# The w_down product of a two-layer encoder as seven half-size products, on one Trainium2 core

## The chip, the cores and the metric

The kernel runs on one core of one Trainium2 chip. A core has TensorE (PE in the profile; its weight loads are shown apart as PEld), VectorE (DVE), ScalarE (ACT), GpSimd (POOL) and SyncE (SP), which issues most DMAs. The metric is the device time of one execution in microseconds; differences are judged by the median of several runs.

## The reference

Two layers over 512 tokens of width 1024. Each layer adds an attention mixer and then a squared-relu MLP; a final RMSNorm follows. Layer 0's mixer joins forgetting attention and chunked attention with a relative bias; layer 1's joins stick-breaking attention and latent attention. The change is in the MLP:

```python
def rmsnorm(x, g):
    xf = x.astype(jnp.float32)
    y = xf * lax.rsqrt(jnp.mean(xf * xf, axis=-1, keepdims=True) + EPS)
    return (y * g.astype(jnp.float32)).astype(x.dtype)

def squared_relu_mlp(h, w_up, w_down):
    return jnp.square(jax.nn.relu(h @ w_up)) @ w_down

for layer in range(DEPTH):
    h = rmsnorm(x, norm_mix[layer])
...
    x = x + squared_relu_mlp(rmsnorm(x, norm_mlp[layer]), w_up[layer], w_down[layer])
return rmsnorm(x, norm_final)
```

All is float32; w_up is 1024 by 4096 and w_down 4096 by 1024 in each layer.

## The kernel before, in words

**Precision.** Every operand of a matmul is split into a high part (a cast to float32r) and the rest: ScalarE casts, VectorE subtracts (`load_w`, lines 429 to 461, for weights). `mm3` (line 423) then issues three matmuls: high by high, high by low, low by high. A matmul loads 128 by 128 elements and streams up to 512 columns into a bank of PSUM.

**Tiles.** X, the residual, is four token tiles of 128 by 1024. `norm_T` (line 533) multiplies X by the gain and transposes it on TensorE into eight chunks of 128 features by 512 tokens. For the MLP it leaves out the token's own scale: it returns one over the mean square for each token tile, and `add_proj` multiplies by it when it adds into X.

**The MLP** (`mlp`, line 753) goes over eight groups of four chunks of the 4096 hidden features. `up_group` makes a group: for each pair of 128-feature blocks two loads of w_up (512 KB each), then for each block 8 chunks by three matmuls; ScalarE takes the relu from the bank, VectorE multiplies it by the bank's relu again, and the square is split. `add_proj` (line 723) multiplies a group by its rows of w_down: for each half of the 1024 columns and each token tile, 4 chunks by three matmuls, and VectorE adds the bank into X with the scale. `up_group` of the next group is recorded ahead of `add_proj` of this one.

**What sets the order.** The program doesn't issue instructions directly: `Plan` (lines 58 to 226) records them, works out their dependencies, and lays them out by a list schedule: on each engine the ready operation of the lowest record number goes first (`urgent` lowers that by `BOOST`). Its clock is a table of durations (`Op.cost`, line 302) and of latencies between engines. A tile is placed only when its pool has a free buffer and, save in pool `u`, when all tiles of its tag that were recorded earlier have been placed. Each engine then runs its instructions in that order, whatever the chip does.

**Buffers.** `wp` holds the halves of weights (tags `wh` and `wl`, four each) and two raw tiles; `tp` seven tiles of 128 by 512 for transposed attention weights; `low_keys` are three tiles that live for the whole program (line 481); `ex` three scratch tiles; PSUM's eight banks are three `mm`, two `sc`, two `tr`, one `av`.

Nearly every instruction is issued from line 225, so the profile's groups are told apart by the names of tiles: `wh`, `wl` are halves of weights, `wr` raw weights, `u` activations, `mm` a bank of a projection, `ex` scratch, `p`, `k`, `pt` attention weights.

Of the kernel before, what the change touches and what calls it, by code (L numbers as in the profile page):

```python
# [17 lines left out]
P = 128  # L18
S = 512
# [3 lines left out]
EPS = 1e-6  # L23
BOOST = 4000
WARM = 60
WARM2 = 12
# [260 lines left out]
class Op:  # L287
# [38 lines left out]

# [44 lines left out]
def trunk(ctx, tc, x, positions, norm_mix, norm_mlp, norm_final, w_in_ab, b_forget, rel_bias,  # L371
# [50 lines left out]

    def mm3(ps, a, b, first, last):

        nc.tensor.matmul(ps, lhsT=a[0], rhs=b[0], start=first, stop=False)
        nc.tensor.matmul(ps, lhsT=a[0], rhs=b[1], start=False, stop=False)
        nc.tensor.matmul(ps, lhsT=a[1], rhs=b[0], start=False, stop=last)

    def load_w(view, parts=None, place="w", raw_place="w"):


        n = int(np.prod(view.shape[1:]))
        if raw_place == "hd":
            raw = hp.tile([P, 1024], F32, tag="hd", name=nm("wr"))
        else:
            raw = wp.tile([P, 1024], F32, tag="wr", name=nm("wr"), bufs=2)
        if place == "hd":
            hi, lo = (hp.tile([P, 1024], F32R, tag="hd", name=nm(s)) for s in ("wh", "wl"))
        elif place == "pt":
            hi, lo = (tp.tile([P, S], F32R, tag="pt", name=nm(s)) for s in ("wh", "wl"))  # L440
        else:
            hi = wp.tile([P, 1024], F32R, tag="wh", name=nm("wh"))
            lo = wp.tile([P, 1024], F32R, tag="wl", name=nm("wl"))
# [32 lines left out]
    for _ in range(WARM):  # L476
        nc.tensor.matmul(warm[:, 0:P], lhsT=idle, rhs=idle, start=True, stop=True)

    low_keys = [cp.tile([P, 2, S], F32R, name=f"KL{i}") for i in range(3)]
    for t in low_keys:
        nc.gpsimd.memset(t[64:128, 0].bitcast(F32), 0.0)
        nc.vector.memset(t[0:64, 1].bitcast(F32), 0.0)

# [51 lines left out]
    def norm_T_(X, g_row, scaled=True, g=None, after=None):  # L537
# [3 lines left out]
        hT = [(utile(), utile()) for _ in range(NC // 2)]  # L541
        stats = []
        for t in range(NT):
# [138 lines left out]
    def attend(ptiles, vw, pr, par):  # L682
# [5 lines left out]
        for b, js in enumerate(((0,), (1, 3), (2,))):  # L688
# [5 lines left out]
            w = widths[b]  # L694
            h = tp.tile([P, S], F32R, tag="pt", name=nm("pt"))[:, :w]
            l = tp.tile([P, S], F32R, tag="pt", name=nm("pt"))[:, :w]
            nc.scalar.copy(h, banks[b][:, :w])
# [24 lines left out]

    def add_proj(X, aT, count, w, k0, scales=None, last=False):

# [8 lines left out]
        def part(wb, half, t):  # L733
            ps = token_proj(lambda c: (wb[c // 2][0][:, c % 2], wb[c // 2][1][:, c % 2]), aT, t, k, S)
            xs = X[t][:, 512 * half:512 * half + 512]
            if scales is None:
                nc.vector.tensor_tensor(xs, ps, xs, ALU.add)
            else:
                nc.vector.scalar_tensor_tensor(xs, ps, scales[t], xs, ALU.mult, ALU.add)

# [6 lines left out]
        else:  # L747
            for half in range(2):
                wb = load(half)
                for t in range(NT):  # L750
                    part(wb, half, t)

    def mlp(X, g_row, wu, wd, ahead=None):

        hT, inv_ms = norm_T(X, g_row, scaled=False)

        def up_group(g):
            act = []
            for pr in range(2):
                n0 = 512 * g + 256 * pr  # L760
                w = [load_w(rows(wu, 4 * i, 4 * i + 4, n0, n0 + 256)) for i in range(2)]
                wc = lambda m: lambda c: tuple(h[:, c % 4, m * P:m * P + P] for h in w[c // 4])
                if g == 0 and pr == 0:
                    pss = [mm_ps(), mm_ps()]
                    for q0 in (0, 256):
                        for m in range(2):
                            for c in range(NC):
                                mm3(pss[m][:, q0:q0 + 256], wc(m)(c), tuple(h[:, q0:q0 + 256] for h in hT[c]),
                                    c == 0, c == NC - 1)
                else:  # L770
                    pss = [feature_proj(wc(m), hT, NC) for m in range(2)]
                for ps in pss:
                    r = etile()
                    nc.scalar.activation(r, ps, AF.Relu)
                    nc.vector.scalar_tensor_tensor(r, ps, 0.0, r, ALU.max, ALU.mult)
                    a = utile()
                    nc.scalar.copy(a[:, 0], r)
# [4 lines left out]
        NG = 8  # L782
        act = up_group(0)
        for g in range(NG):
            if g + 2 == NG and ahead is not None:
                ahead()
            nxt = up_group(g + 1) if g + 1 < NG else None
            add_proj(X, act, 4, wd, 4 * g, inv_ms, last=nxt is None)
            act = nxt

# [149 lines left out]
    def first_of_layer_1():  # L940
        early["v"] = [col_blocks(w_in_cd, NC, 1024, 256, [(4, "hd"), (4, "hd")]),
                      col_blocks(w_in_cd, NC, 1280, 256, [(4, "hd"), (2, "pt")])]

# [27 lines left out]


    hT = norm_T(X, norm_mix[1:2, :])
    xs_dram = dp.tile([NT, P, D], F32, name="xs")
# [87 lines left out]
    def step(name):  # L1062
        nonlocal vw, cq, ck, cqT, ckT, KR, o, wq, wkv
        kind, i = name.rstrip("01234567"), int(name[-1]) if name[-1].isdigit() else None
        if kind == "v":
            first, last = early["v"]
            tail = col_blocks(w_in_cd[6 * P:], 2, 1280, 256, [(2, "pt")])
            vw, _ = v_proj(w_in_cd, 1024, hT, w={0: first, 1: lambda c: last(c) if c < 6 else tail(c - 6)})
# [116 lines left out]
```

## Time and profile before

| | |
|---|---|
| median of 3 runs | 1234.19 us (1233.38 to 1234.39) |
| the profiled execution's own time | 1235.89 us |
| its span in the trace | 1234.2 us |
| granted TensorE clock, mean | 0.995 |
| matmuls in the trace | 6094 |
| loads of w_up, of w_down | 64 and 64, 512 KB each |
| mean DMA rate | 104 GB/s |

The page gives busy time of each engine and its share of the span; "the chain" is the work that ended last, followed back from the end, so what isn't on it cost nothing in that execution. A matmul's own record is longer than its turn on TensorE, because matmuls are pipelined; its turn is read from a run of matmuls on the chain divided by their number. In rows by form, the number after "x" is the count, then busy us, mean ns of one, and the engine's idle time just before with what ended it. Rows of the timeline begin with start and duration in us.

### The profile page before, as it was taken

To read this page: it belongs to the slowest core of one execution; us is meant where nothing else is said; L and a number is where in the kernel's file an instruction comes from. 1 tells how busy PE (TensorE), PEld (TensorE's weight loads), DVE (VectorE), ACT (ScalarE), POOL (GpSimd) and SP (SyncE) were. 2 spreads that over 40 slices of the span, in tenths; PEclk is the share of its full clock that TensorE was granted. 3 is DMA by queue.
4 is the path that set the end of the run, shared out by engine and by line. 5 is a ranking of instruction groups with operands and counts; after the bars stand their busy time and mean duration, and the time that the engine had idled before them with its cause. 6 is when DMAs were issued, how large, how long until landed. Compare 5 with 4: busy or idle time off the path is not lost.

```text
span 1234.2 us, 16494 instructions
## 1 busy us (share of the span) xinstructions
PE 1205.1 (98%) x6094; PEld 1014.8 (82%) x6094; DVE 742.9 (60%) x1307; ACT 537.2 (44%) x990; POOL 157.0 (13%) x290
## 2 busy tenths in 40 slices
PE   8999999999999999999999988999999999999997
PEld 8987878898888888888899766788888888888886
DVE  6457777775454444467633899778744444454444
ACT  6356776444233223333424666565542233233223
POOL 2217322100000000000001466122000000000000
PEclk9999999999999999999999999899999999999999
DMA  6543335123323323343323312691333233323331
GB/s 204 144 103 95 81 91 180 61 94 102 102 90 100 97 90 102 102 135 120 113 75 99 77 52 67 147 240 53 90 99 95 93 102 102 96 85 100 95 102 69
DMA packets 101312, 127.90 MB, mean 104 GB/s; under 512 B 5272, under 2 KB 71200, under 8 KB 101232
## 3 DMA queue, kind: packets, MB, share of 16 engines
q1 hardware_dynamic: 101056, 126.55, 34.6%
q8 instruction: 48, 0.79, 0.3%
q0 software_dynamic: 176, 0.30, 0.1%
q14 instruction: 32, 0.26, 0.1%
HBM read 113.16 MB, written 4.23 MB: 95 GB/s over the span
## 4 chain that ended last, share of the span: by engine, by line
PE 86%; DVE 5%; POOL 3%; DMA 2%; issue 2%; ACT 2%; SPq 0%; POOLq 0%; ACTq 0%; DVEq 0%
PE mm L225 78%; PE tr L225 3%; PE sc L225 3%; POOL p L225 2%; PE av L225 2%; DMA Qm<-u 1%; DVE k L225 1%; DVE wl L225 1%; DVE u L225 1%; DVE pt L225 1%; DMA X<-in_x_dram 1%; DMA wr<-in_w_out_cd_dram 1%; DVE ex L225 0%; ACT p L225 0%; ACT pt L225 0%
## 5 line engine op out<-in xcount | busy, mean ns | idle before, releaser
L225 PE MATMUL mm<-wh,u 128*128 128x512 f32 (+4 forms) x1808 | 512.5, 365 | 0.0
L225 PE MATMUL mm<-u,wh 128*128 128x512 f32 (+1 forms) x1524 | 467.6, 384 | 1.0 <-DVE ex L225 1.0
L225 PEld LDWEIGHTS mm<-wh,u 128*128 128x128 f32 x1808 | 325.4, 189 | 49.0 <-ACT wh L225 0.2
L225 ACT CAST wh<-wr 128x1024 fp32r<-128x1024 f32 (+5 forms) x202 | 201.2, 999 | 322.5 <-PE mm L225 290.2
L225 DVE TENSOR_TENSOR wl<-wr,wh 128x1024 fp32r<-128x1024 f32 (+5 forms) x202 | 234.6, 1164 | 167.4 <-ACT wh L225 166.5
L225 PE MATMUL mm<-wl,u 128*128 128x512 f32 (+4 forms) x904 | 329.2, 364 | 0.0
L225 PEld LDWEIGHTS mm<-u,wh 128*128 128x128 f32 x1524 | 280.2, 188 | 51.7 <-DVE ex L225 1.4
L225 PE MATMUL mm<-u,wl 128*128 128x512 f32 (+1 forms) x762 | 292.4, 384 | 0.0
L225 PEld LDWEIGHTS mm<-wl,u 128*128 128x128 f32 x904 | 170.8, 189 | 24.5 <-DVE wl L225 0.2
L225 PEld LDWEIGHTS mm<-u,wl 128*128 128x128 f32 x762 | 143.7, 189 | 25.2
L225 DVE SCALAR_TENSOR_TENSOR X<-mm,sm,X 128x512 f32<-128x512 f32 x128 | 96.0, 750 | 103.4 <-PE mm L225 103.1
L225 DVE SCALAR_TENSOR_TENSOR ex<-mm,ex 128x512 f32<-128x512 f32 x64 | 44.0, 688 | 78.1 <-ACT ex L225 78.1
L225 ACT ACTIVATE ex<-mm 128x512 f32<-128x512 f32 x64 | 38.0, 594 | 95.5 <-PE mm L225 95.5
L225 POOL TENSOR_SCALAR p<-p,sm 128x128 f32<-128x128 f32 (+1 forms) x96 | 54.8, 571 | 175.7 <-DVE sm L225 155.0
L225 PE MATMUL tr<-ident,p 128*128 128x128 f32 x320 | 62.5, 279 | 13.2 <-POOL p L225 9.6
L225 ACT CAST u<-ex 128x512 fp32r<-128x512 f32 x67 | 41.6, 621 | 66.2 <-DVE ex L225 66.2
L225 POOL TENSOR_TENSOR sm<-sm,mhalf 128x1 f32<-128x1 f32 x20 | 12.0, 599 | 454.3 <-DVE sm L225 454.3
L225 PEld LDWEIGHTS tr<-ident,p 128*128 128x128 f32 x320 | 40.8, 141 | 32.2 <-POOL p L225 16.8
L225 PE MATMUL av<-pt,u 128*128 128x512 f32 (+3 forms) x256 | 65.0, 341 | 1.2 <-DVE pt L225 1.0
L225 ACT ACTIVATE p<-p,sm 128x128 f32<-128x128 f32 (+1 forms) x96 | 54.1, 564 | 26.3 <-DVE sm L225 20.8
L225 DVE TENSOR_TENSOR u<-ex,u 128x512 fp32r<-128x512 f32 x67 | 46.5, 694 | 31.6 <-ACT u L225 31.6
L225 ACT CAST pt<-tr 128x512 fp32r<-128x512 f32 (+1 forms) x96 | 48.1, 513 | 30.2 <-PE tr L225 29.6
(97 smaller groups left out, 897.6 us busy)
## 6 DMA issues: line engine op xcount, KB each, us to landing
wr<-in_w_up_dram SPq DMA_DIRECT2D x64, 512.0 KB, 4.0
wr<-in_w_down_dram SPq DMA_DIRECT2D x64, 512.0 KB, 3.4
wr<-in_w_in_ab_dram SPq DMA_DIRECT2D x22, 512.0 KB, 4.1
wr<-in_w_in_cd_dram SPq DMA_DIRECT2D x11, 512.0 KB, 3.9
X<-in_x_dram SPq DMA_DIRECT2D x8, 512.0 KB, 6.4
wr<-in_w_out_ab_dram SPq DMA_DIRECT2D x8, 512.0 KB, 3.6
wr<-in_w_out_cd_dram SPq DMA_DIRECT2D x8, 512.0 KB, 5.2
KH<-KH SPq DMA_DIRECT2D x24, 128.0 KB, 2.7
```

The costliest lines, as they stand in the source:

```text
L225: getattr(getattr(self.nc, op.engine), op.method)(*op.args, **op.kw)
```

## The change

The hidden features are taken in four groups of eight chunks. For the first three, `seven_products` multiplies the group's activations (512 tokens by 1024) by its rows of w_down (1024 by 1024) as two-by-two blocks with Strassen's identity in the form with fifteen sums: seven products of half the size each way, where eight would be the plain way. A product is four chunks by two token blocks by three matmuls of 512 columns. Sums and differences of the operands are made in float32, most of them in place: those of activations on VectorE (eight instructions a group), those of weights on GpSimd (sixteen), and `page_split` then splits each operand. Products one, three, five and seven accumulate in the same two banks (`main`), and VectorE adds the banks into X after each of them, so a bank is read between products; products two and four share two more (`second`), the sixth has its own. The generator yields after each product, and `mlp` records w_up pairs of the next group after products 2, 4, 6 and 7. In the third group, only the first four blocks of the last group come between, after product 2. The fourth group runs as before, with `add_proj`.

Since activations must be summed before they are split, the token scale moves: `norm_T` now makes a row of reciprocal roots (on GpSimd, then transposed by TensorE into a bank and copied), and the relu step on VectorE multiplies by it; ScalarE then squares. Raw rows of w_down, transposed attention weights and the low keys share one ring of nine 4 KB tiles (`rp`, tag `rd`); the two tags of weight halves become one of eight tiles. The planner's durations (`Op.cost`) get new figures for all engines, which touches the order of the whole program.

```diff
         if self.engine == "tensor":
             if self.method == "transpose":
                 return 109.0
-            cold = 2.0 if self.outs[0].tensor.name.startswith("warm") else 1.0
-            return cold * max(int(np.prod(self.outs[0].shape[1:])) / 2.4, 54.0 if cold > 1.0 else 107.0) + 2.6
+            m = int(np.prod(self.outs[0].shape[1:]))
+            if self.outs[0].tensor.name.startswith("warm"):
+                return 107.0
+            return max(m / 2.4 + 13.5, 107.0)
         psum = any(a.space == bass.MemoryType.PSUM for a in self.ins)
         if self.engine == "scalar":
-            c = n / 1.2 + (52.0 if psum else 93.0)
+            c = n / 1.2 + (155.0 if n < 1024 else 140.0)
             if self.method == "activation" and isinstance(self.kw.get("bias"), bass.AP):
                 c += 93.0
-            return c + (93.0 if "accum_out" in self.kw else 0.0)
+            return c + (188.0 if "accum_out" in self.kw else 0.0)
         if self.engine == "vector":
-            if self.method in ("tensor_copy", "tensor_scalar") and not psum:
-                return n / 1.92 + 70.0
-            return n / 0.96 + 70.0
+            if self.method in ("tensor_copy", "tensor_scalar", "memset") and not psum:
+                return n / 1.92 + 100.0
+            return n / 0.96 + (150.0 if n < 1024 else 100.0) + (83.0 if "accum_out" in self.kw else 0.0)
         if self.method == "tensor_tensor":
-            return 464.0 if n == 1 else 2.1 * n + 150.0
+            return 599.0 if n == 1 else 2.1 * n + 150.0
         if self.method == "affine_select":
-            return 244.0
-        return 0.84 * n + (245.0 if self.method == "tensor_scalar" else 35.0)
+            return 430.0
+        return 0.84 * n + (290.0 if self.method == "tensor_scalar" else 100.0)
 
 
 class Slot:
...
-    wp = pool("wp", bufs=4)
+    wp = pool("wp", bufs=8)
-    tp = pool("tp", bufs=7)
+    rp = pool("rp", bufs=RAW)
...
                 nc.scalar.activation(junk.bitcast(BF16), X[t], AF.Square, accum_out=ss)
-                v = small(1)
-                nc.vector.tensor_scalar(v, ss, 1.0 / D, EPS, ALU.mult, ALU.add)
-                r = small(1)
-                nc.vector.reciprocal(r, v)
-                stats.append(r)
+                r = rstd_of(ss, D)
+                rb = etile()
+                nc.vector.tensor_copy(rb[:, 0:P], r.broadcast_to([P, P]))
+                nc.tensor.transpose(rows_ps[:, t * P:(t + 1) * P], rb[:, 0:P], ident)
         chunks = [(hi[:, k], lo[:, k]) for hi, lo in hT for k in range(2)]
-        return chunks if scaled else (chunks, stats)
+        if scaled:
+            return chunks
+        rstd = cp.tile([P, S], F32, tag="bias", name=nm("rstd"), bufs=2)
+        nc.scalar.copy(rstd, rows_ps)
...
+    def page_split(src, tile_of):
+        both = tile_of()
+        h, l = both[:, 0:S], both[:, S:2 * S]
+        shape = lambda v: v if len(src.shape) == 2 else v.rearrange("p (c n) -> p c n", c=src.shape[1])
+        nc.scalar.copy(shape(h), src)
+        nc.vector.tensor_tensor(shape(l), src, f32(shape(h)), ALU.subtract)
+        return shape(h), shape(l)
+    def seven_products(X, R, wd, k0):
+        lo_t, hi_t = slice(0, 256), slice(256, 512)
+        raw = []
+        for i in range(4):
+            pair = []
+            for c in (i, 4 + i):
+                r = rp.tile([P, 1024], F32, tag="rd", name=nm("rw"))
+                nc.sync.dma_start(r, wd[(k0 + c) * P:(k0 + c + 1) * P, :])
+                pair += [r[:, 0:S], r[:, S:2 * S]]
+            raw.append(pair)
+        a11, a21 = ([R[j][:, :, q] for j in range(2)] for q in (lo_t, hi_t))
+        a12, a22 = ([R[2 + j][:, :, q] for j in range(2)] for q in (lo_t, hi_t))
+        b11, b12, b21, b22 = ([p[k] for p in raw] for k in range(4))
+        acts = lambda v: [page_split(x, lambda: hp.tile([P, 1024], F32R, tag="hd", name=nm("sa"))) for x in v]
+        weights = lambda v: [page_split(x, lambda: wp.tile([P, 1024], F32R, tag="w", name=nm("sw"))) for x in v]
+        def combine(eng, out, x, y, op):
+            for o, p, q in zip(out, x, y):
+                eng.tensor_tensor(o, p, q, op)
+        def spare(like):
+            v = [etile() for _ in like]
+            return [t if len(x.shape) == 2 else t.rearrange("p (c n) -> p c n", c=x.shape[1])
+                    for t, x in zip(v, like)]
+        def product(banks, A, B, first):
+            for i in range(4):
+                for q in range(2):
+                    a = tuple(h[:, i % 2, q * P:(q + 1) * P] for h in A[i // 2])
+                    mm3(banks[q], a, B[i], first and i == 0, i == 3, skip_group_check=not first)
+        def add(banks, row, col):
+            for q in range(2):
+                xs = X[2 * row + q][:, col * S:(col + 1) * S]
+                nc.vector.tensor_tensor(xs, banks[q], xs, ALU.add)
+        V, G = nc.vector, nc.gpsimd
+        main = [ps_sc.tile([P, S], F32, tag="sc", name=nm("pa")) for _ in range(2)]
+        side = lambda: [ps_tr.tile([P, S], F32, tag="tr", name=nm("pb")) for _ in range(2)]
+        A = acts(a11)
+        product(main, A, weights(b11), True)
+        add(main, 0, 0)
+        yield
+        s3 = spare(a11)
+        combine(V, s3, a11, a21, ALU.subtract)
+        A = acts(s3)
+        B = []
+        for i in range(4):
+            t3 = spare(b11[:1])
+            combine(G, t3, b22[i:i + 1], b12[i:i + 1], ALU.subtract)
+            B += weights(t3)
+        second = side()
+        product(second, A, B, True)
+        add(second, 1, 1)
+        yield
+        combine(V, a21, a21, a22, ALU.add)
+        combine(V, a11, a21, a11, ALU.subtract)
+        combine(G, b12, b12, b11, ALU.subtract)
+        combine(G, b11, b22, b12, ALU.subtract)
+        A = acts(a11)
+        product(main, A, weights(b11), False)
+        add(main, 1, 0)
+        yield
+        combine(G, b11, b21, b11, ALU.subtract)
+        A = acts(a22)
+        product(second, A, weights(b11), False)
+        add(second, 1, 0)
+        yield
+        A = acts(a21)
+        product(main, A, weights(b12), False)
+        add(main, 1, 1)
+        yield
+        third = side()
+        A = acts(a12)
+        product(third, A, weights(b21), True)
+        add(third, 0, 0)
+        yield
+        combine(V, a11, a12, a11, ALU.subtract)
+        A = acts(a11)
+        product(main, A, weights(b22), False)
+        add(main, 0, 1)
+        yield
...
+            for ps in pss:
+                r = etile()
+                nc.vector.scalar_tensor_tensor(r, ps, 0.0, rstd, ALU.max, ALU.mult)
+                yield r
+
+        def up_raw(g, pr, R):
+            for m, r in enumerate(up_pair(1024 * g + 256 * pr, first=(g == 0 and pr == 0))):
+                nc.scalar.activation(R[pr][:, m], r, AF.Square)
+
+        def up_split(n0):
...
+        R = squares()
+        for pr in range(4):
+            up_raw(0, pr, R)
+        for g in range(3):
+            steps = seven_products(X, R, wd, 8 * g)
+            nxt = squares() if g < 2 else None
+            act = []
+            for pr, n in enumerate((2, 2, 2, 1)):
+                for _ in range(n):
+                    next(steps)
+                if nxt is not None:
+                    up_raw(g + 1, pr, nxt)
+                elif pr == 0:
+                    act = up_split(3072)
+            for _ in steps:
+                pass
+            R = nxt
+        nxt = up_split(3584)
+        if ahead is not None:
+            ahead()
+        add_proj(X, act, 4, wd, 24)
+        add_proj(X, nxt, 4, wd, 28, last=True)
```

More of the change, by code (lines that the diff above doesn't have):

```diff
@@ L24 @@
 BOOST = 4000
+RAW = 9
 WARM = 60
@@ L421, in move, with mm3 @@
         nc.sync.dma_start(f32(dst), f32(src))
[L423 to L427, printed above, removed]
+    def mm3(ps, a, b, first, last, **kw):
+        nc.tensor.matmul(ps, lhsT=a[0], rhs=b[0], start=first, stop=False, **kw)
+        nc.tensor.matmul(ps, lhsT=a[0], rhs=b[1], start=False, stop=False, **kw)
+        nc.tensor.matmul(ps, lhsT=a[1], rhs=b[0], start=False, stop=last, **kw)
     def load_w(view, parts=None, place="w", raw_place="w"):
@@ L438, in load_w @@
             hi, lo = (hp.tile([P, 1024], F32R, tag="hd", name=nm(s)) for s in ("wh", "wl"))
-        elif place == "pt":
-            hi, lo = (tp.tile([P, S], F32R, tag="pt", name=nm(s)) for s in ("wh", "wl"))
-        else:
-            hi = wp.tile([P, 1024], F32R, tag="wh", name=nm("wh"))
-            lo = wp.tile([P, 1024], F32R, tag="wl", name=nm("wl"))
+        elif place == "rd":
+            both = rp.tile([P, 2, S], F32R, tag="rd", name=nm("wb"))
+            hi, lo = both[:, 0], both[:, 1]
+        else:
+            hi, lo = (wp.tile([P, 1024], F32R, tag="w", name=nm(s)) for s in ("wh", "wl"))
         dst = raw[:, :n]
@@ L477, in trunk, with make_low_keys @@
         nc.tensor.matmul(warm[:, 0:P], lhsT=idle, rhs=idle, start=True, stop=True)
[L481 to L484, printed above, removed]
+    low_keys = []
+    def make_low_keys():
+        low_keys[:] = [rp.tile([P, 2, S], F32R, tag="rd", name=nm("KL")) for _ in range(3)]
+        for t in low_keys:
+            nc.gpsimd.memset(t[64:128, 0].bitcast(F32), 0.0)
+            nc.vector.memset(t[0:64, 1].bitcast(F32), 0.0)
+    make_low_keys()
     def strip():
@@ L541, in norm_T_ @@
         hT = [(utile(), utile()) for _ in range(NC // 2)]
-        stats = []
+        rows_ps = None if scaled else ps_av.tile([P, S], F32, tag="av", name=nm("rs"))
         for t in range(NT):
@@ L694, in attend @@
             w = widths[b]
-            h = tp.tile([P, S], F32R, tag="pt", name=nm("pt"))[:, :w]
-            l = tp.tile([P, S], F32R, tag="pt", name=nm("pt"))[:, :w]
+            both = rp.tile([P, 2, S], F32R, tag="rd", name=nm("pt"))
+            h, l = both[:, 0, :w], both[:, 1, :w]
             nc.scalar.copy(h, banks[b][:, :w])
@@ L721, in o_store, with add_proj @@
         return (oT[:, 0], oT[:, 1])
-    def add_proj(X, aT, count, w, k0, scales=None, last=False):
+    def add_proj(X, aT, count, w, k0, last=False):
         k = count
@@ L735, in part @@
             xs = X[t][:, 512 * half:512 * half + 512]
[L736 to L739, printed above, removed]
+            nc.vector.tensor_tensor(xs, ps, xs, ALU.add)
         if last:
@@ new lines, in mlp, with up_pair @@
+    def mlp(X, g_row, wu, wd, ahead=None):
+        hT, rstd = norm_T(X, g_row, scaled=False)
+        def up_pair(n0, first=False):
+            w = [load_w(rows(wu, 4 * i, 4 * i + 4, n0, n0 + 256)) for i in range(2)]
+            wc = lambda m: lambda c: tuple(h[:, c % 4, m * P:m * P + P] for h in w[c // 4])
+            if first:
+                pss = [mm_ps(), mm_ps()]
+                for q0 in (0, 256):
+                    for m in range(2):
+                        for c in range(NC):
+                            mm3(pss[m][:, q0:q0 + 256], wc(m)(c), tuple(h[:, q0:q0 + 256] for h in hT[c]),
+                                c == 0, c == NC - 1)
+            else:
+                pss = [feature_proj(wc(m), hT, NC) for m in range(2)]
+            for ps in pss:
[6 more added lines that the diff above has]
+        def up_split(n0):
@@ L758, in up_group @@
             act = []
             for pr in range(2):
[L760 to L775, printed above, removed]
+                for r in up_pair(n0 + 256 * pr):
                     a = utile()
+                    nc.scalar.activation(r, r, AF.Square)
                     nc.scalar.copy(a[:, 0], r)
@@ L780, in up_group, with squares @@
             return act
[L782 to L789, printed above, removed]
+        def squares():
+            return [up.tile([P, 2, S], F32, tag="u", name=nm("sq")) for _ in range(4)]
+        R = squares()
[20 more added lines that the diff above has]
+        add_proj(X, nxt, 4, wd, 28, last=True)
     def load_x(src, late=None, between={}):
@@ L970, in trunk @@
     nc.vector.tensor_scalar(sinT[64:128], sinT[64:128], -1.0, None, ALU.mult)
+    make_low_keys()
     hT = norm_T(X, norm_mix[1:2, :])
@@ L1172 @@
     laid['consts'] = shape_constants()
-    nc = _bacc.Bacc("TRN2", target_bir_lowering=False, num_devices=1, dynamic_dma_scratch_size=8192)
+    nc = _bacc.Bacc("TRN2", target_bir_lowering=False, num_devices=1, dynamic_dma_scratch_size=4096)
     arrays, args = {}, []
```

7 lines of the change are left out of this document (3 added, 4 removed).

## The prediction

> **What bounds the kernel now.** I read the page first (shares of engines, the chain's summary), then the chain in order of time, then the busy time by stretches.
>
> ```profile
> span 1234.2 us, 16494 instructions
> PE 1205.1 (98%) x6094; PEld 1014.8 (82%) x6094; DVE 742.9 (60%) x1307; ACT 537.2 (44%) x990; POOL 157.0 (13%) x290
> PE 86%; DVE 5%; POOL 3%; DMA 2%; issue 2%; ACT 2%; SPq 0%; POOLq 0%; ACTq 0%; DVEq 0%
> ```
>
> ```profile
> 235.85 20.66 PE mm L225 x91
> ...
> 270.08 335.91 PE mm L225 x1512
> ...
> 881.89 342.27 PE mm L225 x1540
> ```
>
> ```profile
> core 0: us, PE busy (x) PEld busy (x) DVE busy (x) ACT busy (x) POOL busy (x), PEclk, DMA share, GB/s
> 84.00:236.00 152.00, 147.34 (x783) 120.66 (x783) 117.80 (x316) 103.47 (x236) 57.99 (x110) 1.00 0.35 103
> 270.00:606.00 336.00, 336.00 (x1515) 279.57 (x1515) 174.63 (x216) 110.37 (x139) 1.20 (x2) 1.00 0.34 106
> 674.00:860.00 186.00, 172.25 (x907) 140.38 (x907) 157.42 (x323) 121.02 (x293) 78.99 (x136) 0.97 0.41 105
> 890.00:1220.00 330.00, 330.00 (x1458) 273.33 (x1457) 159.84 (x192) 102.52 (x132) 1.10 (x2) 1.00 0.30 94
> ```
>
> The kernel has two kinds of stage. In the two MLPs (270 to 606 and 890 to 1220) the chain is one unbroken run of matmuls, 335.91 and 342.27 us long: nothing but TensorE sets the time, VectorE is busy 174.63 of 336 us, ScalarE 110.37, GpSimd 1.20. In the two attention stretches (84 to 236, 674 to 860) TensorE has idle time of its own, 152.00 − 147.34 = 4.7 and 186.00 − 172.25 = 13.8 us, 18.4 together, and VectorE is nearly as busy as it. The change takes matmuls out of the first kind of stage and pays in VectorE, ScalarE and GpSimd there; by its new durations it reorders the second kind. One 512-wide matmul costs TensorE 20.66 / 91 = 0.227 us.
>
> **Matmuls removed.** A group of eight chunks of w_down took 8 chunks × 4 token blocks × 2 halves × 3 terms = 192 matmuls. Each of the seven products takes 4 × 2 × 3 = 24, the same in shape (128 rows loaded, 512 columns), so the group takes 168. Three groups in each of two layers: 6 × 24 = 144 fewer, and 144 × 0.227 = 32.7 us less. As the chain lies on TensorE through the whole stage, all of this counts, so long as the other engines keep up.
>
> **What the other engines get.** The durations are those of the groups by form:
>
> ```profile
> L225 DVE TENSOR_TENSOR wl<-wr,wh 128x1024 fp32r<-128x1024 f32 x177 | 217.2, 1228 | 162.5 <-ACT wh L225 162.1
> ...
> L225 DVE TENSOR_TENSOR u<-ex,u 128x512 fp32r<-128x512 f32 x67 | 46.5, 694 | 31.6 <-ACT u L225 31.6
> ...
> L225 DVE SCALAR_TENSOR_TENSOR ex<-mm,ex 128x512 f32<-128x512 f32 x64 | 44.0, 688 | 78.1 <-ACT ex L225 78.1
> ...
> L225 ACT CAST u<-ex 128x512 fp32r<-128x512 f32 x67 | 41.6, 621 | 66.2 <-DVE ex L225 66.2
> ...
> L225 DVE TENSOR_TENSOR X<-mm,X 128x512 f32<-128x512 f32 x48 | 32.6, 687 | 6.6 <-PE mm L225 5.7 <-DMA X<-xs 0.5
> ...
> L225 DVE TENSOR_TENSOR ex<-X,gain 128x512 f32<-128x512 f32 x16 | 10.7, 680 | 0.1
> ...
> L225 POOL TENSOR_TENSOR p<-p,k 128x511 f32<-128x511 f32 x8 | 9.1, 1141 | 4.6 <-DVE k L225 4.5
> ```
>
> A product splits four weight blocks and two activation tiles of 512 elements (six subtractions like u<-ex,u, 0.694) and adds two banks into X (like X<-mm,X, 0.687): 6 × 0.694 + 2 × 0.687 = 5.54 us of VectorE, against 24 × 0.227 = 5.45 of TensorE. A pair of w_up blocks costs two weight splits and two relu steps, 2 × 1.228 + 2 × 0.688 = 3.83 us, against 48 × 0.227 = 10.9. The sums and differences of operands are eight on VectorE (0.680 each, 5.4) and sixteen on GpSimd (1.141 each, 18.3). A full group (seven products, four pairs) is then 7 × 5.54 + 4 × 3.83 + 5.4 = 59.5 us of VectorE and 18.3 of GpSimd beside 7 × 5.45 + 4 × 10.9 = 81.7 of TensorE. ScalarE has one cast of 0.621 per split, less than VectorE everywhere. So VectorE stays below TensorE on average (59.5 of 81.7, where it was 174.63 of 336), and by itself the average costs nothing.
>
> **Where the average doesn't hold.** The third group has only four blocks of w_up between its second and third products, and then products three to seven stand in a row: TensorE 5 × 5.45 = 27.2 us, VectorE 5 × 5.54 + 6 × 0.680 = 31.8, an excess of 4.6. How far the splits can run ahead is set by free weight tiles:
>
> ```profile
> ACT wh L225 <- PE mm L225: 290.2, 139, 8.5
> ```
>
> Already now the casts wait 290.2 us for matmuls to give tiles back; eight tiles of one tag hold two products' weights. So I count 4.6 us in each layer, 9.2 in all. The second cost is two engines in each other's way. These rows show instructions that ran side by side:
>
> ```profile
> 687.94 2.10 DVE L225 TENSOR_TENSOR wl<-wr,wh 128x1024 fp32r<-128x1024 f32 x1
> ```
>
> ```profile
> 687.87 1.09 POOL L225 TENSOR_TENSOR p<-p,k 128x511 f32<-128x511 f32 x1
> ```
>
> ```profile
> 170.95 1.73 POOL L225 TENSOR_SCALAR p<-p,sm 128x512 f32<-128x512 f32 x1 [2.07 <-DVE sm L225]
> ```
>
> ```profile
> 170.97 1.24 DVE L225 TENSOR_TENSOR wl<-wr,wh 128x1024 fp32r<-128x1024 f32 x1 [0.18 <-ACT wh L225]
> ```
>
> ```profile
> L225 POOL TENSOR_SCALAR p<-p,sm 128x512 f32<-128x512 f32 x24 | 20.4, 849 | 31.6 <-DVE sm L225 28.0 <-PE sc L225 3.7
> ```
>
> The split that began 0.07 us after GpSimd's multiply took 2.10 us, where its group's mean is 1.228: it ended about one 1.09 later. The GpSimd scaling at 170.95 took 1.73 us beside a VectorE split of 1.24, where its group's mean is 0.849. So a GpSimd sum and a VectorE split queue behind each other, and nearly all the new work (splits, sums) is of these two kinds. The Trainium skill says this of the chip (SBUF — State Buffer, section "Who interferes with whom"): a VectorE instruction with two SBUF inputs contends with a GpSimd instruction that reads SBUF, and the later one is blocked until the first has finished; the 2.10 us agree, and by that rule the two engines' times in the products must be added, which is the sum of the third rival.
>
> With both added, a full group is 59.5 + 18.3 = 77.8 us, still under 81.7. The third group up to its seventh product, with VectorE 7 × 5.54 + 5.4 + 4 × (1.228 + 0.688 + 0.694) = 54.7, is 73.0 against 7 × 5.45 + 21.8 = 60.0, 13.0 us over, 26 in both layers. GpSimd runs free beside the X additions and relu steps, whose one input is a bank, and in VectorE's idle time, so I stay with 9.2, near the end where lookahead works, and keep 0 and 26 as the bounds of this term within my forecast.
>
> **Smaller edits.** The scale moves from the X additions (0.750 to 0.687 each) into the relu step: off the path. The row of reciprocal roots costs eight transposes of 0.11 us:
>
> ```profile
> 868.31 0.44 PE tr L225 x4
> ```
>
> that is +0.9. The first relu now waits for the statistics of all four token tiles; 96 half-wide matmuls of the first pair cover that. If they didn't, GpSimd's power, copy, transposes and ScalarE's copy would add some 2 us per layer. Loads of w_down keep their number and bytes (3.4 us each); the next group's eight come while the last pairs (10.9 each) and the seventh product run, as blocks of the raw ring are given back from product five on; if all waited for product seven's splits, eight in turn at 3.4 us are 27.2 against 10.9 + 5.45 + 10.9 = 27.3 of cover, so nothing. SP's queue also carries the w_up loads, and no other queue is passed. Sine and cosine of layer 1 share two tiles with the new row and move behind the last pair of layer 0; 192 matmuls (43.6 us) follow to cover them.
>
> ```profile
> wr<-in_w_down_dram SPq DMA_DIRECT2D x64, 512.0 KB, 3.4
> ```
>
> **The reset durations** touch every engine's order. The new figures lie near these rows (VectorE on 1024: 1167 for 1.228 us, before 1137; a matmul 226.8 for 0.227 us, before 215.9), and the transposed weights of attention get six pairs of buffers beside the low keys where there were three and a half. Attention's 18.4 us of idle TensorE bound a gain; I take as much again for the loss, and zero for the sum, because rows of before can't show an order that wasn't run.
>
> **Sum.** The profiled execution took 1235.89 us (span 1234.2 and 1.7 around it), the median of the runs is 1234.19, that is 1.7 lower. 1235.89 − 32.7 + 9.2 + 0.9 = 1213.3; less 1.7 gives 1211.6 us.
>
> **Rivals.** First, nothing stalls and attention gives back half its idle time: 1211.6 − 9.2 − 9.2 = 1193.2. For: whole groups fit even when both engines are added. Against: the third group's five products. Second, the new order loses in attention: 1211.6 + 18.4 = 1230.0. For: 674 to 860 has VectorE at 157.42 of 186, so a changed order has little slack. Against: durations nearer to the rows. Third, slower: GpSimd and VectorE exclude each other and buffers allow no work ahead of its stretch. Then products three and four with their pair cost 2 × 5.54 + 3.83 + 4 × 0.680 + 12 × 1.141 = 31.3 us against 21.8, 9.5 over, in two groups, and the third group 13.0: 32.0 per layer, 64 in all, and 1211.6 − 9.2 + 64 = 1266.4. It decides, and eats the whole gain, from half its price, about 32 us of stalls. For: the 2.10 us. Against: GpSimd's first two differences need only loaded weights, so they can run during products one and two.
>
> **Numbers.** Forecast 0.57 (1211.6; its own 1202 to 1228 by the bounds 0 and 26), first rival 0.16, second 0.15, third 0.12. Differences under 0.2%, some 2.5 us, can't be told from no change. The forecast, the first and most of the second rival lie below 1231.7: faster 0.84; a second rival that loses a little more gives same 0.04; the third slower 0.12. Leaving out the third and the low part of the first, the range is 1195 to 1232.
>
> **What would show it.** Right: about 144 fewer 512-wide matmuls at 0.227 us, MLP stretches about 11 to 16 us shorter each, VectorE busy near 70% there and GpSimd some 55 us per layer, idle TensorE only between products three and seven of the third group, splits of 0.694 stretched to over 1.5 where they meet a GpSimd sum. Wrong: TensorE gaps in every group whose releaser is GpSimd or a split; gaps ended by a w_down load; or MLPs as forecast and attention longer or shorter by more than 5 us.

## The result, and the profile after

The changed kernel took 1274.32 us in the median of four runs (1267.19 to 1279.54), against 1233.79 for the kernel before in its four: a ratio of 1.0327 (95% interval 1.0304 to 1.035). It is slower by 40 us. The profiled execution is the fastest of the four, 1267.19 us with a span of 1265.5, so its trace accounts for 31 of the 40 us, and what the other three lost beyond it no trace shows. These are the first lines of its page, and the chain's summary:

```profile
span 1265.5 us, 16788 instructions
PE 1195.4 (94%) x5958; PEld 994.0 (79%) x5958; DVE 902.8 (71%) x1502; ACT 604.6 (48%) x1148; POOL 331.6 (26%) x397
PE 58%; DVE 13%; POOL 2%; issue 2%; DMA 2%; ACT 1%; POOLq 0%; ACTq 0%; DVEq 0%
```

TensorE has 136 fewer matmul records (144 fewer products' matmuls, eight more transposes), and VectorE's share of the chain rose from 5% to 13%. (This chain is followed back only to 273.91 us, so its shares add up to 78% of the span.) The same two stretches of time as before, both inside the MLPs, by engine (the columns are those of the prediction's table):

```profile
270.00:606.00 336.00, 314.71 (x1371) 255.23 (x1371) 249.37 (x303) 137.61 (x210) 84.80 (x53) 0.98 0.28 89
890.00:1220.00 330.00, 311.74 (x1378) 253.78 (x1377) 238.99 (x293) 136.75 (x216) 84.46 (x51) 0.97 0.25 80
```

TensorE now idles 21.3 and 18.3 us there, where it idled not at all. The chain in order of time (start, us, what) shows the place. It breaks where the last w_up pair ahead of product one ends:

```profile
275.73 36.52 PE mm L226 x177
312.27 1.89 DVE ex L226 x3
314.16 1.70 DVE sq L226
315.87 2.30 DVE sa L226 x2
318.17 1.67 DVE sw L226
319.84 1.20 DVE X L226 x2
321.63 1.85 DVE sw L226 x2
```

Here are the stretches of product one, product two, the w_up pair behind it, and product three, cut at the first matmul of each:

```profile
core 0: us, PE busy (x) PEld busy (x) DVE busy (x) ACT busy (x) POOL busy (x), PEclk, DMA share, GB/s
312.07:317.51 5.44, 5.44 (x25) 4.50 (x24) 5.24 (x6) 2.45 (x4) 3.23 (x2) 1.00 0.00 0
317.51:329.70 12.19, 9.03 (x25) 6.08 (x24) 12.19 (x11) 4.37 (x6) 12.00 (x8) 0.72 0.00 0
329.70:343.68 13.98, 11.46 (x49) 8.86 (x48) 13.98 (x14) 6.55 (x12) 11.01 (x7) 1.00 0.27 76
343.68:349.12 5.44, 5.44 (x25) 4.50 (x24) 5.44 (x8) 2.33 (x4) 0.76 (x1) 1.00 0.00 0
```

Product two takes 12.19 us for 5.44 us of matmuls, the pair behind it 13.98 for 10.88, and VectorE is busy in every microsecond of both. All six groups look like this and nothing else in them does: product two takes 12.19, 12.19, 13.37, 13.80, 12.19 and 13.33 us, products one and three to seven take 5.44 each. Cut the same way, the excess of the six second products is 44.4 us and of the six pairs (a double pair in the third group) 14.3, together 58.7. The start of each MLP, from the first w_up matmul to the end of four pairs, is 49.1 and 47.7 us where it was 45.5: 5.8 more. The stretch ahead of the first MLP is 1.8 shorter, the attention of layer 1 1.6 longer. With the forecast's 32.7 us of matmuls saved: 58.7 + 5.8 − 1.8 + 1.6 − 32.7 = 31.6, and the span grew by 1265.5 − 1234.2 = 31.3.

What VectorE and GpSimd do in those 26 us, from the timeline of each (start, us, instruction, idle time before and what ended it):

```profile
312.27 0.69 DVE L226 SCALAR_TENSOR_TENSOR ex<-mm,rstd 128x512 f32<-128x512 f32 x1 [4.75 <-PE mm L226]
...
318.09 1.75 DVE L226 TENSOR_TENSOR sw<-ex,sw 128x512 fp32r<-128x512 f32 x1
...
321.56 3.45 DVE L226 TENSOR_TENSOR sw<-ex,sw 128x512 fp32r<-128x512 f32 x2
...
326.61 1.77 DVE L226 TENSOR_TENSOR sw<-ex,sw 128x512 fp32r<-128x512 f32 x1
```

```profile
313.70 1.61 POOL L226 TENSOR_TENSOR ex<-rw,rw 128x512 f32<-128x512 f32 x1 [42.01 <-ACT sq L226]
315.40 1.62 POOL L226 TENSOR_TENSOR rw<-rw 128x512 f32<-128x512 f32 x1
317.70 5.06 POOL L226 TENSOR_TENSOR ex<-rw,rw 128x512 f32<-128x512 f32 x3 [0.69 <-PE pa L226]
322.72 5.11 POOL L226 TENSOR_TENSOR rw<-rw 128x512 f32<-128x512 f32 x3
327.80 6.91 POOL L226 TENSOR_TENSOR rw<-rw,rw 128x512 f32<-128x512 f32 x4
```

Two things are to be seen. GpSimd stood idle for 42.01 us and began its first difference only after the last relu step (ex<-mm,rstd at 312.27 and ScalarE's square of it): the difference is written to a scratch tile (`ex`), and `Plan` places the tiles of that ring in recorded order, so product two's scratch comes after the last pair's. Its inputs were there: given tiles of their own (e3 below), these differences ran ahead of product one. And once they run together, each VectorE split takes 1.7 us instead of 0.694, each GpSimd sum 1.6 to 1.7 instead of 1.1. They take turns: 1.09 and 0.68 make 1.77. The Trainium skill has this in SBUF — State Buffer, section "Who interferes with whom": a VectorE instruction with two SBUF inputs contends with a GpSimd instruction that reads SBUF, and the ports that the two share are an exclusive lock; the 1.75 to 1.77 us of the splits agree.

### The profile page after: what moved, and what is told of

Read it like the earlier page. It is cut to its first block, busy times and chain, and to the rows that moved or that the text cites. A ratio compares the mean times of both kernels' runs of the same rounds, so it can differ in the third digit from the quotient of the medians.

```text
span 1265.5 us, 16788 instructions
## 1 busy us (share of the span) xinstructions
PE 1195.4 (94%) x5958; PEld 994.0 (79%) x5958; DVE 902.8 (71%) x1502; ACT 604.6 (48%) x1148; POOL 331.6 (26%) x397
## 4 chain that ended last, share of the span: by engine, by line
PE 58%; DVE 13%; POOL 2%; issue 2%; DMA 2%; ACT 1%; POOLq 0%; ACTq 0%; DVEq 0%
PE mm L226 41%; PE pa L226 8%; PE pb L226 5%; DVE sq L226 3%; DVE sw L226 2%; POOL p L226 2%; DVE wl L226 2%; PE tr L226 2%; DVE ex L226 1%; PE sc L226 1%; DVE sa L226 1%; PE av L226 1%; DVE k L226 1%; DVE X L226 1%; DMA wr<-in_w_in_cd_dram 1%
## 5 line engine op out<-in xcount | busy, mean ns | idle before, releaser
L226 PE MATMUL mm<-wh,u 128*128 128x512 f32 (+4 forms) x1008 | 267.6, 348 | 2.1 <-ACT u L226 2.0
L226 PEld LDWEIGHTS mm<-wh,u 128*128 128x128 f32 x1008 | 176.5, 190 | 21.8 <-ACT u L226 2.3
L226 PE MATMUL mm<-wl,u 128*128 128x512 f32 (+4 forms) x504 | 175.9, 349 | 0.3 <-DVE wl L226 0.2
L226 PE MATMUL pb<-sw,sa 128*128 128x512 f32 x432 | 120.1, 431 | 25.1 <-DVE sw L226 25.0
L226 PE MATMUL pa<-sw,sa 128*128 128x512 f32 x576 | 134.5, 389 | 0.0
L226 PEld LDWEIGHTS pb<-sw,sa 128*128 128x128 f32 x432 | 87.9, 208 | 54.4 <-DVE sw L226 36.3
L226 PEld LDWEIGHTS pa<-sw,sa 128*128 128x128 f32 x576 | 108.1, 188 | 22.5
L226 DVE TENSOR_TENSOR sw<-rw,sw 128x512 fp32r<-128x512 f32 x144 | 103.8, 750 | 19.3 <-ACT sw L226 19.2
L226 ACT CAST sw<-rw 128x512 fp32r<-128x512 f32 x144 | 86.7, 620 | 61.9 <-PE mm L226 19.8
L226 POOL TENSOR_TENSOR rw<-rw,rw 128x512 f32<-128x512 f32 x48 | 85.4, 1805 | 28.8 <-DVE sw L226 28.8
```

Source lines behind the costliest of these rows:

```text
L226: getattr(getattr(self.nc, op.engine), op.method)(*op.args, **op.kw)
```

## The experiments

The theory was that the loss sits in product two, from a late start (**A**) and from taking turns (**B**). Rivals were the reset durations (**C**), and weight tiles or VectorE's load as such (**D**). Product two's times are read from the starts of matmuls. "Stalls of the six groups" is the excess of all products and pairs over 0.227 us a matmul, added up: 58.7 us in the changed kernel.

| run | median us | ratio to before (95%) | product two, us |
|---|---|---|---|
| changed kernel | 1274.3 | 1.0327 (1.0304 to 1.035) | 12.2 to 13.8 |
| e1 durations alone | 1236.9 | 1.0021 (1.0006 to 1.0037) | none |
| e2 no third difference | 1212.0 | 0.9831 (0.9809 to 0.9853) | 5.44 |
| e3 early | 1227.9 | 0.9963 (0.9945 to 0.9981) | 6.7 to 9.5 |
| e4 difference on VectorE | 1253.4 | 1.0169 (1.0147 to 1.0192) | 12.6 to 13.6 |
| e5 pairs after 1, 3, 5, 7 | 1351.1 | 1.0956 (1.0924 to 1.0988) | 15.4 to 18.6 |
| e7 all sums on VectorE | 1234.1 | 1.0007 (0.9989 to 1.0024) | 7.1 |
| e8 early, all on VectorE | 1243.5 | 1.0074 (1.0049 to 1.0099) | 8.5 to 10.1 |
| e9 early, pairs after 1, 3, 5, 7 | 1288.2 | 1.0445 (1.0409 to 1.048) | 8.8 to 11.1 |
| e10 both differences early | 1212.1 | 0.9824 (0.9811 to 0.9838) | 5.44 |
| e11 the same, all on VectorE | 1211.0 | 0.982 (0.98 to 0.984) | 5.44 |
| e12 e10 and a tile for the root | 1211.7 | 0.9824 (0.9809 to 0.984) | 5.44 |
| e13 old durations | 1281.7 | 1.04 (1.0386 to 1.0414) | 16.4 to 17.3, two of the pair's matmuls inside |

### The durations, one way and the other

In e1 only `Op.cost` of the changed kernel was put into the kernel before; in e13 the old `Op.cost` was put back into the changed kernel.

> The kernel before with the new planner durations alone. Theory A (the loss sits in product two: GpSimd's four differences b22 - b12 start late and then take turns with VectorE): outside the MLPs little moved in the changed kernel (-1.8 us up to the first MLP, +1.6 us between the MLPs), so this runs within 4 us of before, 1230 to 1238. Theory C (the reset durations give a worse order): 1250 or more.

> The changed kernel with the planner's old durations. If the reset durations have no part in the loss, product two still takes 12 to 14 us in every group and the time is 1260 to 1285. If they cause the late differences, product two falls under 8 and the time under 1245.

e1: 1236.88 us, 0.2% over before; e13: 1281.66 us, and the stall is there, longer than with the new durations even without the two matmuls of the pair that fall into it (product two of the first group):

```profile
317.69:334.54 16.85, 8.92 (x27) 5.77 (x26) 16.85 (x13) 6.45 (x10) 16.32 (x10) 0.87 0.00 0
```

The reset durations are some 3 us of loss in the old kernel and, in the changed one, no cause of the 40: without them it is 7 us slower still. As the cause of the stall, C falls.

### Without the difference

```diff
-        for i in range(4):
-            t3 = spare(b11[:1])
-            combine(G, t3, b22[i:i + 1], b12[i:i + 1], ALU.subtract)
-            B += weights(t3)
+        B = weights(b22)
```

> The changed kernel, product two taking b22 itself in place of b22 - b12 (the difference is left out, 24 GpSimd instructions in all). Theory A: product two falls from 12.2 to 13.8 us to under 7 in all six groups and the pair behind it to 10.9; the profiled 1267.2 less about 58 gives 1205 to 1215. Theory D (free weight tiles or VectorE's load hold up product two, whatever GpSimd does): product two stays over 10 us and the time over 1255.

The kernel leaves the difference out, so it computes something else; it serves for its time alone. It took 1212.00 us, product two 5.44 us in all six groups and the pair behind it 10.88:

```profile
319.42:324.86 5.44, 5.44 (x26) 4.50 (x24) 5.44 (x8) 2.31 (x4) 0.00 (x0) 1.00 0.39 106
324.86:335.74 10.88, 10.88 (x50) 9.01 (x48) 10.88 (x13) 5.17 (x10) 6.63 (x4) 1.00 0.13 45
```

The weight splits, their tiles and twelve of the sixteen GpSimd sums are all still there, and so is the activation difference in the scratch ring. So these four differences are where the whole stall hangs, and D falls.

### The difference early

```diff
-            t3 = spare(b11[:1])
+            both = hp.tile([P, 1024], F32, tag="hd", name=nm("t3"))
+            t3 += [both[:, 0:S], both[:, S:2 * S]]
...
+        combine(G, t3, b22, b12, ALU.subtract)
+        B = weights(t3)
```

> The changed kernel with the four differences b22 - b12 in two tiles of the ring of split activations, not in the scratch ring that the relu steps of the last pair use too. Theory A, start time deciding: GpSimd makes them during the seventh product and the pair before, product two falls to 5.4 to 7 us, the time to 1205 to 1225. Theory B (turn-taking of GpSimd and VectorE decides, whenever they start): product two stays over 10 us and the time over 1250.

1227.89 us, 0.4% faster than before, and product two takes 6.7 to 9.5 us, mostly between the two expectations. GpSimd now began the first group's differences 41 us ahead of product one (313.96):

```profile
272.42 5.98 POOL L226 TENSOR_TENSOR t<-rw,rw 128x512 f32<-128x512 f32 x4
```

VectorE's timeline shows what is left (third group of layer 0; product one began at 480.96):

```profile
481.16 0.69 DVE L226 SCALAR_TENSOR_TENSOR ex<-mm,rstd 128x512 f32<-128x512 f32 x1 [4.75 <-PE mm L226]
481.77 3.23 DVE L226 TENSOR_TENSOR ex<-sq 128x512 f32<-128x512 f32 x2
...
488.52 2.48 DVE L226 TENSOR_TENSOR sw<-t,sw 128x512 fp32r<-128x512 f32 x4
```

VectorE idles 4.75 us for the last relu step, and only then makes the activation difference (ex<-sq), which is in the same scratch ring. A late start again, of the other operand. In this group GpSimd's sums for product three ran beside it, so the two activation differences took 3.23 us where two take 1.28 without them (e9 below). In the first group GpSimd was idle in this stretch, and product two still took 6.69.

### The difference on VectorE, and all sums on VectorE

```diff
-            combine(G, t3, b22[i:i + 1], b12[i:i + 1], ALU.subtract)
+            combine(V, t3, b22[i:i + 1], b12[i:i + 1], ALU.subtract)
```

> The changed kernel with the four differences b22 - b12 on VectorE, in the same scratch ring. Theory B (turn-taking decides): each block costs 0.69 + 0.69 us of VectorE in place of two turns of some 1.7, product two falls to 6 to 9 us, the time to 1225 to 1245. Theory A, start time deciding: they still begin behind the last relu, product two stays near 10 to 12 us, the time over 1250.

1253.44 us, product two 12.6 to 13.6. By the expectation this speaks for A alone, and that reading is wrong: GpSimd did not leave the stretch, its later sums moved up into it, and the four weight splits still took 1.75 to 1.77 us each:

```profile
320.81 4.97 POOL L226 TENSOR_TENSOR rw<-rw 128x512 f32<-128x512 f32 x3 [2.48 <-DVE ex L226]
325.73 5.65 POOL L226 TENSOR_TENSOR rw<-rw,rw 128x512 f32<-128x512 f32 x3
```

So e7 took GpSimd out altogether (`V, G = nc.vector, nc.vector`), scratch as it was.

> The changed kernel with all sums on VectorE, none on GpSimd, scratch ring as it was. Theory B (taking turns lengthens each step from 0.69 to 1.7 us): no split is stretched any more; from the last relu step VectorE has some 14 steps of 0.67 us, 9.4 us, product two falls to 5.9 to 8 us and the time to 1212 to 1232, although VectorE has 10.9 us more work in a group. Theory A (late start alone): product two stays 10 to 13 us and the time over 1245.

1234.06 us, just over the range expected, and product two 7.1 in all six groups. Products three and four of the first two groups now take 6.7 and 7.9, the latter with four of the next pair's matmuls inside. Its stretches of products one and two and VectorE's groups there:

```profile
312.17:317.61 5.44, 5.44 (x26) 4.51 (x24) 4.79 (x8) 2.44 (x4) 0.00 (x0) 1.00 0.00 0
317.61:324.74 7.13, 6.03 (x25) 4.35 (x24) 7.13 (x11) 3.73 (x5) 0.00 (x0) 1.00 0.02 5
```

```profile
L226 DVE TENSOR_TENSOR sw<-ex,sw 128x512 fp32r<-128x512 f32 x4 | 2.6, 688 | 0.0
L226 DVE TENSOR_TENSOR ex<-rw,rw 128x512 f32<-128x512 f32 x4 | 2.6, 686 | 0.0
```

Eleven VectorE instructions took 12.19 us in the changed kernel's stretch, eleven (not all the same ones) take 7.13 here; a split of product two is 0.688 where it was 1.75. VectorE has more work in each group and the kernel is 40 us faster than the changed one. In the traces the stalls of the six groups fall from 58.7 to 21.1 us, 10.1 of it in product two and 11.0 in products three and four with their pairs. B is shown: with the late start as it is, taking turns costs some 38 us of the 58.7.

### Pairs in other places

```diff
-            for pr, n in enumerate((2, 2, 2, 1)):
+            for pr, n in enumerate((1, 2, 2, 2)):
```

> The changed kernel with the pairs of w_up recorded after products 1, 3, 5 and 7 (after 1 in the third group) in place of 2, 4, 6 and 7. If product two waits only because its sums can't start before the last relu step of the previous pair, the 10.9 us of the pair between cover it: product two 5.4 us everywhere. The eight sums for product three then have less room: product three 5.4 to 9 us. Time 1205 to 1235. If GpSimd and VectorE taking turns is too much in total, the stall only moves to product three, of 10 us or more, and the time stays over 1250.

1351.09 us, the slowest of all; product two takes 15.4 to 18.6 us, and the pair ahead of it and product three stall as well. The pair between covers nothing, because it is recorded ahead of product two, so its relu steps come first in the scratch ring as well. GpSimd now waited for the last relu step of that next pair, 18 us after product one began (312.97):

```profile
330.92 1.58 POOL L226 TENSOR_TENSOR ex<-rw,rw 128x512 f32<-128x512 f32 x1 [58.29 <-ACT sq L226]
```

> b22 - b12 in its own tiles on GpSimd, and the pairs of w_up after products 1, 3, 5 and 7. Product two 5.4 us everywhere; product three at most 7; time 1203 to 1220. If what is left in the early version (product two 6.7 to 9.5 us) is VectorE's queue behind the last relu step, the pair between covers it; if it is taking turns in total, product three grows by as much as product two falls.

1288.23 us: with the weight difference early, the activation difference is still in the scratch ring and is made right behind the next pair's last relu step; products two (8.8 to 11.1) and three (9.1 to 10.4) both stall:

```profile
331.04 0.69 DVE L226 SCALAR_TENSOR_TENSOR ex<-mm,rstd 128x512 f32<-128x512 f32 x1 [4.75 <-PE mm L226]
331.64 1.28 DVE L226 TENSOR_TENSOR ex<-sq 128x512 f32<-128x512 f32 x2
```

In both runs the expectation that the pair covers product two failed, and both bear out A: the start goes with the scratch ring's order, wherever the pair stands.

### Early and on VectorE

> Both: all sums on VectorE, and b22 - b12 in its own tiles so that it can be made early. If late start and taking turns are two separate causes, the two gains add up until product two reaches 5.4 us: product two 5.4 to 6.5, time 1205 to 1218. If VectorE's load becomes the bound (70 us of 82 in a group), other products grow over 5.44.

1243.54 us, 9.5 us over e7: the gains did not add up. VectorE made the difference after the last relu step although it no longer needs the scratch ring (product one began at 314.33):

```profile
314.53 0.69 DVE L226 SCALAR_TENSOR_TENSOR ex<-mm,rstd 128x512 f32<-128x512 f32 x1 [4.75 <-PE mm L226]
...
320.59 1.89 DVE L226 TENSOR_TENSOR t<-rw,rw 128x512 f32<-128x512 f32 x3
322.39 2.49 DVE L226 TENSOR_TENSOR sw<-t,sw 128x512 fp32r<-128x512 f32 x4
```

Its order on VectorE is the plan's, and there it stands behind the activation difference, which still had to wait: its tiles have the tag `hd`, recorded behind those for the split of that difference, and `Plan` places a tag's tiles in recorded order. On GpSimd, in e3, nothing stood ahead of it in the engine's own order. A ring of its own lets an operation start early; the plan decides whether it does.

Why e8 is slower than e7 is to be seen in the same rows. Here all four differences are made ahead of the first weight split, which began at 322.39, 8.1 us after product one; in e7 they alternate, and the first split began 3.8 us after product one (312.17):

```profile
315.98 0.69 DVE L226 TENSOR_TENSOR sw<-ex,sw 128x512 fp32r<-128x512 f32 x1
```

So TensorE waited 3.12 us in one piece in e8, 1.12 and 0.76 in e7. Behind that wait, in four groups of six, six to eight of e8's matmuls came 0.40 to 0.59 us apart in place of 0.227. The stalls of the six groups are 30.4 us against e7's 21.1.

### Both differences early

```diff
-        s3 = spare(a11)
+        s3 = [otile().rearrange("p (c n) -> p c n", c=2) for _ in a11]
```

on top of e3; e11 has all sums on VectorE besides; e12 has the broadcast root of `norm_T_` in the tile ring `p0` in place of `etile()`.

> Product two's activation difference (a11 - a21) too leaves the scratch ring, for the two tiles of the ring that is idle in the MLP; b22 - b12 stays early, on GpSimd. In the early version VectorE sat idle for 4.75 us ahead of the last relu step and then had 9.7 us of work in a row. If the scratch ring's order is the cause of what is left, product two falls from 6.7 to 9.5 us to 5.4 to 6.5 us and the time from 1228 to 1210 to 1222. If instead the splits' weight tiles decide, product two stays as it was and so does the time, 1224 to 1232.

> The same with all sums on VectorE. Taking turns is gone too: if it still costs something, product two and three are 5.4 us and the time is 3 to 8 us under the run with GpSimd, 1205 to 1218. If VectorE's own load is now the bound, the time is over that run's.

> Both differences early on VectorE and GpSimd, and at the start of each MLP the broadcast reciprocal root in a tile of its own instead of a scratch tile. The stretch from the first w_up matmul to the end of four pairs, 45.5 us before and 47.7 to 50.2 in the changed kernels, should fall to 46 to 48; the time 2 to 5 us under the run without it.

e10: 1212.05 us, and every product in all six groups takes 5.44:

```profile
314.83:320.27 5.44, 5.44 (x26) 4.51 (x24) 5.24 (x8) 3.78 (x6) 0.00 (x0) 1.00 0.00 0
320.27:325.71 5.44, 5.44 (x26) 4.50 (x24) 5.04 (x7) 3.84 (x7) 1.51 (x2) 1.00 0.66 192
325.71:336.59 10.88, 10.88 (x50) 9.01 (x48) 9.67 (x13) 2.81 (x5) 4.84 (x3) 1.00 0.01 2
```

```profile
L226 POOL TENSOR_TENSOR rw<-rw,rw 128x512 f32<-128x512 f32 x24 | 42.8, 1806 | 59.7 <-DVE sw L226 59.7
L226 POOL TENSOR_TENSOR t<-rw,rw 128x512 f32<-128x512 f32 x12 | 19.8, 1678 | 96.9 <-DVE sq L226 96.9
```

These GpSimd sums still take 1.7 to 1.8 us, so the engines still take turns, and it costs nothing: the work now begins in the pair before or earlier, where there is room. e11 measures the same (1210.95; the intervals overlap), so its expected 3 to 8 us are not there. In e12 the start of the MLPs is 48.4 and 47.3 us against 51.1 and 48.2 in e10, as expected in direction, but not under 46 to 48 in the first layer, and the time (1211.70) can't be told from e10's. All three beat both kernels, by 1.8% to the kernel before.

## Why the prediction was wrong

**Matmuls removed: right.** 24 matmuls take 5.44 us in every product that doesn't wait, and with the stall gone (e10) the kernel is at 1212.05 us. That this lies so near the forecast's 1211.6 is luck: the 9.2 us counted for the third group aren't there, and the two starts of the MLPs cost 8.3 us (e10) where 0.9 was counted.

**The other engines' averages: right, and beside the point.** VectorE at 249.37 of 336 us is under TensorE, but one stretch of 26 us was full in every group.

**Third group's products three to seven, 9.2 us: wrong.** They take 5.44 each in the changed kernel, and in e10 too; their splits ran ahead. That term should have been nothing.

**Taking turns: right mechanism, wrong overlap.** The step that failed is "GpSimd runs free beside the X additions and relu steps, whose one input is a bank, and in VectorE's idle time, so I stay with 9.2, near the end where lookahead works", with the sentence against the third rival, that the first two differences need only loaded weights and so can run during products one and two. I had looked at weight tiles for what limits lookahead. What limited it was the scratch ring of three tiles, in recorded order, shared with the relu steps: differences could not begin before the last relu step, which ends after product one has begun. That one wait put the six differences in scratch, their splits, the sums in place for product three (eight on GpSimd, four on VectorE) and product one's additions into one stretch. There, with turns of 1.7 us instead of 0.69, 58.7 us of stall came together in six groups, where 9.2 was counted; without the turns it is 21.1 (e7), without the late start nothing (e10). The prediction's own sign of being wrong, gaps in every group that a split ends, came (TensorE waited 25.0 us for splits of these weights). The price of the third rival, 64 us, came near by luck: its place, products three and four, was wrong, for these took 5.44 each.

**Start of the MLPs: mis-sized.** 0.9 us was counted, 5.8 measured, 3.6 in layer 0 and 2.2 in layer 1. With the old durations (e13) the starts take 46.3 and 47.7, so most of layer 0's part goes with the planner's order and layer 1's does not. The root's own tile takes 2.7 and 0.9 us off e10 (e12), but e10's first start is itself 2.0 longer than the changed kernel's. What makes the rest stays open.

**Reset durations: zero was about right.** The attention stretches moved by −1.8 and +1.6 us; the durations alone cost the old kernel 0.2% (e1), and in the changed kernel they gain 7 us (e13).

**The two causes together.** Removing the late starts alone (e10) takes 62 us off the median, removing the turns alone (e7) 40; the two add up to more than the whole stall, because the turns hurt only where the work is late.

## What to carry to other kernels

When work moves to an engine with spare time, ask not only whether its average fits but when its first instruction can start: follow its output tile to its ring, and look at what was recorded ahead of it in that ring. A scratch ring shared with a late producer ties an early operation to that producer. Here two engines that took turns cost nothing while both were early (e10 and e11 measure the same), and some 38 of 58.7 us where both were late.

## What the runs showed of the hardware beside this

The granted clock fell in the second products of the changed kernel, to 0.72, 0.86, 0.87, 0.63, 0.72 and 0.87 in the order of the groups. The pairs behind them waited too (11.46 us busy of 13.98 in the first) and show 1.00. In e3, one group has seven slow matmuls behind a wait of 2.6 us, and three others have the same wait without them. So what pattern of waits brings the clock down these runs don't show. It explains little of the changed kernel's loss: in the first group the last split ended at 328.38, and the five matmuls left ran from 328.44 to 329.70, near their full-speed 0.227 each. From the last split to the end of product two is 1.3 to 1.4 us in five groups, and 1.8 in layer 1's first, at 0.63.
